# One encoder layer on one core: zeros on TensorE ahead of the opening, its first loads on two queues, smaller first pieces, and another order of the attention scores

## The chip, the cores and the metric

One core of one Trainium2 chip runs the whole layer as one program. The metric is the device time of one execution in microseconds. The kernel before took 1105.54 us (median of 3 runs, 1104.93 to 1105.83).

## The reference

The layer works on 256 tokens of width 2048, in float32. Cut to what matters here:

```python
h = rms_norm(x, attn_norm)
proj = h @ w_in                       # 2048 x 6152
qa, ka, va, fa, qb, kb, vb = split(proj)
# group A, 8 heads of 128: c = cumsum(log_sigmoid(fa + b_forget)) over the tokens
logits = qa . ka / sqrt(128) + c[t] - c[s]      # s <= t, then softmax, then @ va
# group B, 8 heads: stick-breaking attention from qb, kb, vb
x = x + concat(rms_norm(out_a), rms_norm(out_b)) @ w_out
x = x + conv_ffn(rms_norm(x))         # up, causal convolution of width 3, SiLU gate, down
```

`rms_norm` divides each token by the root of its mean square and multiplies the columns by a weight. The kernel multiplies by the weight first (as a scale per row of the transposed tokens) and divides by the root at the end of a projection.

## The kernel before, in words

**Arithmetic.** Every large product is done in three passes of matmuls on operands rounded to float32r: weights are cut into a high part `w_hi` (a cast, mostly on ScalarE) and a rest `w_lo` (a subtraction on VectorE), tokens into the two halves of `hT`. The passes are high by high, high by the token's rest, and the weights' rest by high. Small products, such as the attention scores, use plain float32 operands.

**Steps.** The program is a list of steps, each of one weight piece. The main loop at the end of `hybrid_layer` (L1270) runs over the steps n; at n it asks for the weights of step n + 6 (`LOAD`, a transfer on SyncE's queue into one of five buffers `w_raw`), lets the cast and subtraction of step n + 2 be written (`SPLIT`), and writes the matmuls of step n. Each engine, and SyncE's queue, works strictly in the order in which this was written.

**The opening** (`opening`, L322) computes the first 688 columns of the values of group A into four PSUM banks (`acc_v`: two halves of 344 columns by two blocks of 128 tokens). It goes through the 16 tiles of 128 columns of x in nine pieces: two of one tile, then seven of two tiles (`sizes`, L325). For each piece
- `loads` asks for the weights (344 KB a tile, L236) and for the columns of x (`load_x`, L118; 128 KB a tile) listed in `x_loads`. All go on SyncE's queue, x's first piece ahead of the first weights;
- `tokens` transposes the tiles of x on TensorE (`transposed`, L174, into `ps_x`), writes the two halves of `hT` on ScalarE and VectorE (`split_tokens`, L182 and L183) and casts and subtracts the weights (L242, L250). After every fourth tile ScalarE also sums the squares of 512 columns of x (`squares`, L190);
- `matmuls` issues 12 matmuls of 344 columns a tile (L369 for one-tile pieces, L267 for others), and behind them the `tokens` of the piece two further on.

The tokens of the first piece also need the norm's weights as columns: `prow` is loaded as rows on ScalarE's queue (L94, its first instruction), TensorE transposes it into `pp` (L167), VectorE copies it to `ga` (L168), which scales every `hT`. ScalarE's table load (L95) stands behind that transfer. The first two pieces are transposed together, ahead of the first matmul.

**The stage behind the opening** begins on TensorE with a second transpose of parameter rows (again `pp`, L167) and continues with the rest of the values.

**The scores of group A** (`fox_head`, L698): for each of 8 heads, three products accumulate into one bank `ps_s`: queries by keys for the first 128 tokens (L705), for the second 128 (L706), and a product that adds c[t] - c[s] in the form of a selecting row `headR` by the gates' sums `cR` (L707). VectorE then adds the mask and takes maxima (L712 to L715).

Of the kernel before, what the change touches and what calls it, by code (L numbers as in the profile page):

```python
# [9 lines left out]
F32 = mybir.dt.float32  # L10
# [5 lines left out]
P = 128  # L16
D = 2048
S = 256
NT = S // P
KT = D // P  # L20
# [16 lines left out]
C_COLS = C_MF + 4 * P  # L37

LOAD, SUM, SPLIT = 6, 4, 2
STAGGER = 3  # L40
FFN_PARTS = [(f, min(f + 8, NFT)) for f in range(0, NFT, 8)]

# [2 lines left out]
def hybrid_layer(  # L45
# [19 lines left out]
    nc = tc.nc  # L65
    act, dve = nc.scalar, nc.vector
# [16 lines left out]
    psb = ctx.enter_context(tc.tile_pool(name="psb", bufs=4, space=bass.MemoryType.PSUM))  # L83
# [7 lines left out]

    NC2 = 2 * NFT
    prow = const.tile([50, P], F32, name="prow")
    act.dma_start(prow[:KT, :], attn_norm[0].rearrange("(n p) -> n p", p=P))  # L94
    act.preload_act_table_set("natural_log_exp_and_others")  # L95
    cs = const.tile([P, C_MF], F32, name="cs")
    bf = const.tile([P, NH], F32, name="bf")
    pcol = const.tile([P, 50], F32, name="pcol")
    ga = const.tile([P, KT], F32, name="ga")
# [17 lines left out]
    def load_x(k, n, queue=nc.sync):  # L117
        queue.dma_start(x2[:, :, k * P : (k + n) * P], xp[:, :, k * P : (k + n) * P])  # L118

    ident = cs[:, C_ID : C_ID + P]  # L120
    make_identity(nc, ident)
    tri = cs[:, C_TRI : C_TRI + P]
    tri_one = cs[:, C_TRI : C_TRI + 2 * P]
# [41 lines left out]
    def columns(dst, rows, n):  # L165
        pp = psb.tile([P, 512], F32, name="pp", tag="t")
        nc.tensor.transpose(pp[:, :n], rows, ident[:n, :n])  # L167
        dve.tensor_copy(dst, pp[:, :n])  # L168

    def transposed(k, n=2):  # L170
        ps = psb.tile([P, 2, S], F32, name="ps_x", tag="t")
        for j in range(n):
            for t in range(NT):
                nc.tensor.transpose(  # L174
                    ps[:, j, t * P : (t + 1) * P], x2[:, t, (k + j) * P : (k + j + 1) * P], ident
                )
        return ps
# [67 lines left out]
    def split(raw, a, b):  # L245
        return subtracted(raw, *cast(raw, a * b, act.copy), a, b)
# [49 lines left out]
    VC = 344  # L296
# [25 lines left out]
    def opening():  # L322

        banks = []
        sizes = [1, 1] + [2] * 7  # L325
        starts = [sum(sizes[:i]) for i in range(len(sizes))]
        last = len(sizes) - 1
        x_loads = {0: (0, 2), 1: (2, 2), 2: (4, 2), 3: (6, 2), 4: (8, 4), 5: (12, 4)}
        mem = {}

        def piece(i):
            k0, n = starts[i], sizes[i]

            def loads():
                if i == 0:
                    load_x(*x_loads[i])
                mem["raw", i] = load(rows_of(wi, k0, n, V0, 2 * VC))
                if 0 < i < 6:
                    load_x(*x_loads[i])
                if i == 7:  # L340
                    load_parameters()

            def tokens():
                if n == 1 and i == 0:
                    columns(ga, prow[:KT, :], KT)
                    ps, mem["ps"] = (transposed(j, 1) for j in range(2))
                    hi, lo = cast(mem["raw", 0], 2 * VC, dve.tensor_copy)
                    split_tokens(ps, 0, ga, 1)
                    mem["parts", 0] = subtracted(mem["raw", 0], hi, lo, 1, 2 * VC)
                elif n == 1:  # L350
                    split_tokens(mem["ps"], 1, ga, 1)
                    mem["parts", 1] = split(mem["raw", 1], 1, 2 * VC)
                else:
                    split_tokens(transposed(k0), k0, ga)
                    mem["parts", i] = split(mem["raw", i], 2, 2 * VC)
                if k0 % 4 == 2:
                    squares(ss1, k0 // 4)
                if i == last:
                    ready.add("x")

            def matmuls():
                if i == 0:
                    banks.extend([bank_tile(f"acc_v{t}", 2 * j + t) for t in range(NT)] for j in range(2))
                if n == 1:
                    hi, lo = mem["parts", i]
                    for l, w in ((0, hi), (1, hi), (0, lo)):
                        for j in range(2):
                            for t in range(NT):
                                nc.tensor.matmul(  # L369
                                    banks[j][t][:, :VC], of_half(hT[:, k0], l, t),  # L370
                                    w[:, 0, j * VC : (j + 1) * VC], start=i == l == 0 and w is hi, stop=False,
                                )
                else:
                    for j in range(2):
                        in_three(
                            [banks[j][t][:, :VC] for t in range(NT)], mem["parts", i], 2, of_tokens(k0),
                            False, i == last, cut=slice(j * VC, (j + 1) * VC),
                        )
                if i + 2 <= last:
                    tokens_of[i + 2]()  # L380

            tokens_of.append(tokens)

            def follow():
                v = tile_of["v"] = at.tile([P, NT, WF], F32, name="vA", tag="v")
                for j in range(2):
                    for t in range(NT):
                        act.activation(
                            v[:, t, j * VC : (j + 1) * VC], banks[j][t][:, :VC], AF.Identity,
                            scale=rstd1[:, t : t + 1],  # L390
                        )
                    yield

            new_step(loads, None, tokens if i < 2 else None, matmuls, follow if i == last else None)

        tokens_of = []
        for i in range(len(sizes)):
            piece(i)
# [299 lines left out]
    def fox_head(h, half):  # L698
        q, k = tile_of[f"qA{half}"][:, h % 4, :], tile_of[f"kA{half}"][:, h % 4, :]
        v = tile_of["v"]  # L700
        yield
        yield
        ps = psb.tile([P, 512], F32, name="ps_s", tag="t")[:, : 3 * P].rearrange("p (a b) -> p a b", a=3)
        s0, s1 = ps[:, 0, :], ps[:, 1:3, :].rearrange("p a b -> p (a b)")
        nc.tensor.matmul(s0, q[:, :P], k[:, :P], start=True, stop=False)  # L705
        nc.tensor.matmul(s1, q[:, P:], k, start=False, stop=False)  # L706
        nc.tensor.matmul(  # L707
            ps.rearrange("p a b -> p (a b)"), headR[:, h : h + 1].to_broadcast([P, P]), cR, start=False, stop=True
        )
        started["fox"] += 1  # L710
        diagonal = ps[:, 0::2, :]
        dve.tensor_tensor(diagonal, diagonal, maskF, op=ALU.add)  # L712
        nm = small.tile([P, NT], F32, name="nm", tag="nm", bufs=4)
        dve.tensor_reduce(nm[:, 0:1], s0, axis=AX.X, op=ALU.max, negate=True)
        dve.tensor_reduce(nm[:, 1:2], s1, axis=AX.X, op=ALU.max, negate=True)  # L715
        yield
        yield
        l = small.tile([P, NT], F32, name="l", tag="l", bufs=4)
        pr = tmp.tile([P, 3, P], F32, name="pr", tag="pr")
        p0, p1 = pr[:, 0, :], pr[:, 1:3, :].rearrange("p a b -> p (a b)")  # L720
        act.activation(p0, s0, AF.Exp, bias=nm[:, 0:1], accum_out=l[:, 0:1])
        act.activation(p1, s1, AF.Exp, bias=nm[:, 1:2], accum_out=l[:, 1:2])
        rl = small.tile([P, NT], F32, name="rl", tag="rl", bufs=4)
        dve.reciprocal(rl, l)
        dve.tensor_scalar(p0, p0, rl[:, 0:1], None, op0=ALU.mult)
        dve.tensor_scalar(p1, p1, rl[:, 1:2], None, op0=ALU.mult)
        yield
        yield
        pt = psb.tile([P, 512], F32, name="ps_p", tag="t")[:, : 3 * P].rearrange("p (a b) -> p a b", a=3)
        for i in range(3):  # L730
            nc.tensor.transpose(pt[:, i, :], pr[:, i, :], ident)
        yield
        pT = tmp.tile([P, 3, P], F32, name="pT", tag="pT")
        act.copy(pT, pt)
        yield
        po = psb.tile([P, S], F32, name="ps_o", tag="t")
        hs = slice(h * HD, (h + 1) * HD)
        nc.tensor.matmul(po, v[:, 0, hs], pT[:, 0:2, :].rearrange("p a b -> p (a b)"), start=True, stop=False)
        nc.tensor.matmul(po[:, P:], v[:, 1, hs], pT[:, 2, :], start=False, stop=True)
        yield  # L740
        act.activation(oFox[:, h, :], po, AF.Identity, scale=g_fox[:, h : h + 1])
        sq = squared(po, 0, h)
        if sq is not None:
            dve.tensor_tensor(ssq[0], ssq[0], sq, op=ALU.add)
# [595 lines left out]
```

## Time and profile before

| | |
|---|---|
| median of 3 runs | 1105.54 us |
| the profiled execution | 1106.18 us |
| its span, first to last instruction | 1104.4 us |
| TensorE busy | 1092.8 us |
| VectorE busy | 902.9 us |
| ScalarE busy | 741.3 us |
| read from HBM | 252 MB, 230 GB/s over the span |

A page of the profile gives the busy time of each engine, the chain of work that ended last, and the costliest groups of instructions. Its other views list waits by who waited for whom, and instructions in order of time. PE is TensorE's matmul side, PEld its weight loads, DVE VectorE, ACT ScalarE, POOL GpSimd, SP SyncE; a q behind a name is its queue, where transfers are issued. In a row of the view by time stand the start (us from the first instruction), the duration, engine, line of the kernel, operation, output and inputs, and how many instructions are merged in the row; in brackets, the idle time ahead of it and what ended it. Matmuls overlap, so the time that one occupies TensorE is read from start to start.

### The profile page before, as it was taken

The page shows a single profiled execution, that of the slowest core. Times are in us where ns is not written, and L with a number is a line of the kernel's source. Part 1 is how long each engine was busy: PE and PEld are TensorE (multiplying, and loading weights), DVE is VectorE, ACT ScalarE, POOL GpSimd, SP SyncE. Part 2 cuts the span into 40 slices and gives each one's busy share as a digit, 9 for nine tenths or more (in the row PEclk, how much of TensorE's full clock was granted, in tenths as well). Part 3 has the DMA queues.
Part 4 walks back from the last instruction along what each step waited for, and adds up shares of the span by engine and source line. Part 5 has one row for each costly group of instructions (what it writes and reads, how often), then busy time and mean ns, then how long its engine had stood idle before and what let it go on. Part 6 is the DMA issues. An engine that isn't in the chain of part 4 may idle for free.

```text
span 1104.4 us, 14415 instructions
## 1 busy us (share of the span) xinstructions
PE 1092.8 (99%) x5666; PEld 941.5 (85%) x5666; DVE 902.9 (82%) x860; ACT 741.3 (67%) x923; POOL 55.1 (5%) x50
## 2 busy tenths in 40 slices
PE   8999999999999999999999999999999999999998
PEld 7988888888878888888888888888888888888886
DVE  4666888878897576679988998889898898879996
ACT  5745786667666567666767767766776667666762
POOL 0000000000100000000000010000000000000000
PEclk9999999999999999999999999999999999999999
DMA  8856877869777366557979598995979789795994
GB/s 303 285 192 190 262 184 241 208 189 265 255 191 264 125 206 202 185 166 174 316 201 289 203 267 250 249 300 160 301 208 277 237 230 303 197 317 168 287 263 139
DMA packets 174220, 255.35 MB, mean 231 GB/s; under 512 B 4408, under 2 KB 98378, under 8 KB 174154
## 3 DMA queue, kind: packets, MB, share of 16 engines
q1 hardware_dynamic: 152282, 210.26, 56.1%
q0 software_dynamic: 21696, 44.04, 22.6%
q8 instruction: 44, 0.72, 0.3%
q14 instruction: 22, 0.18, 0.0%
q10 hardware_dynamic: 176, 0.14, 0.0%
HBM read 252.33 MB, written 2.10 MB: 230 GB/s over the span
## 4 chain that ended last, share of the span: by engine, by line
PE 92%; DVE 5%; ACT 1%; issue 1%; DMA 0%; DVEq 0%; SPq 0%; ACTq 0%
PE pu L1089 43%; PE bank_a L267 16%; PE bank_b L267 9%; PE acc_o L267 5%; PE bank_c L267 5%; PE bank_p L267 4%; PE acc_v L267 4%; PE acc L267 2%; DVE w_lo L250 2%; PE bank_e L267 2%; ACT w_hi L242 1%; PE ps_x L174 1%; PE ps_h L627 0%; DMA w_raw<-in_w_in_dram 0%; PE acc_v L369 0%
## 5 line engine op out<-in xcount | busy, mean ns | idle before, releaser
L250 DVE TENSOR_TENSOR w_lo<-w_raw,w_hi 128x2048 fp32r<-128x2048 f32 (+2 forms) x246 | 551.9, 2246 | 147.5 <-ACT w_hi L242 146.8
L242 ACT CAST w_hi<-w_raw 128x2048 fp32r<-128x2048 f32 (+2 forms) x245 | 460.2, 1879 | 223.5 <-PE pu L1089 92.7
L1089 PE MATMUL pu<-hT,w_hi 128*128 128x512 f32 x1408 | 334.8, 390 | 0.7 <-ACT w_hi L242 0.7
L1089 PEld LDWEIGHTS pu<-hT,w_hi 128*128 128x128 f32 x1408 | 262.5, 188 | 54.8 <-ACT w_hi L242 1.2
L1089 PEld LDWEIGHTS pu<-hT,w_lo 128*128 128x128 f32 x1408 | 180.6, 191 | 7.0
L1089 PE MATMUL pu<-hT,w_lo 128*128 128x256 f32 x1408 | 182.8, 283 | 0.0
L1019 ACT ACTIVATE tap<-up,ccol 128x256 f32<-128x256 f32 x176 | 74.6, 495 | 0.0
L1138 POOL DMA_DIRECT2D w_raw<-in_w_down_dram x30 | 38.5, 1284 | 720.2 <-DVE w_raw L1156 317.7
L267 PE MATMUL bank_a<-w_hi,hT 128*128 128x512 f32 x160 | 40.7, 396 | 0.0
L267 PE MATMUL bank_b<-w_hi,s 128*128 128x512 f32 x160 | 40.1, 392 | 0.3 <-DVE xb L1111 0.3
L267 PE MATMUL bank_a<-w_hi,g 128*128 128x512 f32 x160 | 40.0, 392 | 0.0
L267 PE MATMUL bank_a<-w_hi,s 128*128 128x512 f32 x160 | 40.0, 392 | 0.0
L267 PEld LDWEIGHTS bank_a<-w_hi,hT 128*128 128x128 f32 x160 | 29.2, 188 | 5.6
L267 PEld LDWEIGHTS bank_b<-w_hi,s 128*128 128x128 f32 x160 | 28.9, 189 | 5.7 <-issue 0.5
L267 PEld LDWEIGHTS bank_a<-w_hi,s 128*128 128x128 f32 x160 | 28.9, 189 | 5.2
L267 PEld LDWEIGHTS bank_a<-w_hi,g 128*128 128x128 f32 x160 | 28.9, 189 | 5.3
L1012 ACT ACTIVATE gate<-up,ccol 128x256 f32<-128x256 f32 x44 | 24.0, 594 | 12.5 <-DVE s L1065 7.4
L1024 DVE TENSOR_TENSOR gate<-gate,tap 128x512 f32<-128x512 f32 x44 | 30.3, 689 | 2.5 <-ACT tap L1019 0.2
L1024 DVE TENSOR_TENSOR val<-val,tap 128x512 f32<-128x512 f32 x44 | 30.3, 689 | 2.3
L1005 DVE TENSOR_TENSOR up<-t,R 128x512 f32<-128x512 f32 x44 | 30.5, 692 | 1.5
L267 PE MATMUL acc_o<-w_hi,oSb 128*128 128x512 f32 x128 | 31.3, 396 | 0.0
L267 PE MATMUL acc_v<-w_hi,hT 128*128 128x344 f32 x176 | 31.2, 323 | 0.0
(269 smaller groups left out, 1392.4 us busy)
## 6 DMA issues: line engine op xcount, KB each, us to landing
w_raw<-in_w_up_dram SPq DMA_DIRECT2D x88, 1024.0 KB, 6.2
w_raw<-in_w_down_dram SPq DMA_DIRECT2D x44, 1024.0 KB, 7.0
w_raw<-in_w_in_dram SPq DMA_DIRECT2D x40, 1024.0 KB, 5.7
w_raw<-in_w_down_dram POOLq DMA_DIRECT2D x30, 1024.0 KB, 9.7
w_raw<-in_w_out_dram SPq DMA_DIRECT2D x16, 1024.0 KB, 7.5
w_raw<-in_w_in_dram POOLq DMA_DIRECT2D x8, 1024.0 KB, 9.7
w_raw<-in_w_in_dram SPq DMA_DIRECT2D x11, 688.0 KB, 7.7
xb<-in_x_dram POOLq DMA_DIRECT2D x4, 512.0 KB, 9.2
```

Source lines behind the costliest of these rows:

```text
L174: nc.tensor.transpose(ps[:, j, t * P : (t + 1) * P], x2[:, t, (k + j) * P : (k + j + 1) * P], ident)
L242: copy(hi[:, :n], raw[:, :n])
L250: dve.tensor_tensor(lo[:, :n], raw[:, :n], f32(hi[:, :n]), op=ALU.subtract)
L267: nc.tensor.matmul(o, lhs(i, l, t), r[:, i, :] if cut is None else r[:, i, cut], start=starts and j == 0, stop=stops and j == 3 * n - 1, s ...
L1005: dve.tensor_tensor(u[:, :, 2:], t2, R, op=ALU.mult)
L1012: act.activation(a[:, j, :], u[:, j, 2:], AF.Identity, scale=ccol[:, 2, f : f + 1], bias=ccol[:, 3, f : f + 1],)
L1019: act.activation(taps[w][:, j, :], u[:, j, w : w + S], AF.Copy, scale=ccol[:, w, f : f + 1])
L1024: dve.tensor_tensor(a, a, tap, op=ALU.add)
L1089: nc.tensor.matmul(acc[:, j, S:] if low else acc[:, j, :], (lo if low else hi)[:, i, j * P : (j + 1) * P], hT[:, k, 0, :] if low else hT[: ...
L1138: nc.gpsimd.dma_start(mem[weights].rearrange("p (a b) -> p a b", a=4), plus, accum_op=ALU.add)
```

## The change

Five edits, four of them in the opening.

1. VectorE sets 128 columns of the tile `junk` to zero at the start, and a new function `idle(n)` lets TensorE multiply them by themselves n times into a bank that nobody reads (`WARM = 7, 4`): seven ahead of the columns of `prow`, four behind the transposes of the first two tiles.
2. x's first piece goes on ScalarE's queue, with `prow` and the table load behind it; the first weights are then first on SyncE's queue.
3. The opening has eleven pieces: six of one tile, then five of two (`sizes`). The loads of x keep their sizes and are spread over pieces 0, 2, 4, 6, 7 and 8.
4. `tokens` is written once for both sizes; squares still come after every fourth tile, and the parameters' loads still stand with tiles 12 and 13.
5. In `fox_head` the gates' product is first and opens the accumulation; the two products of queries and keys follow.

```diff
+WARM = 7, 4
...
-    act.dma_start(prow[:KT, :], attn_norm[0].rearrange("(n p) -> n p", p=P))
-    act.preload_act_table_set("natural_log_exp_and_others")
...
+    dve.memset(junk[:, :P], 0.0)
     make_identity(nc, ident)
...
+    def idle(n):
+        ps = psb.tile([P, 2, S], F32, name="ps_i", tag="t")
+        for _ in range(n):
+            nc.tensor.matmul(ps[:, 0, :P], junk[:, :P], junk[:, :P], start=True, stop=True)
...
-        sizes = [1, 1] + [2] * 7
+        sizes = [1] * 6 + [2] * 5
...
-        x_loads = {0: (0, 2), 1: (2, 2), 2: (4, 2), 3: (6, 2), 4: (8, 4), 5: (12, 4)}
+        x_loads = {0: (0, 2), 2: (2, 2), 4: (4, 2), 6: (6, 2), 7: (8, 4), 8: (12, 4)}
...
                 if i == 0:
+                    load_x(*x_loads[i], act)
+                    act.dma_start(prow[:KT, :], attn_norm[0].rearrange("(n p) -> n p", p=P))
+                    act.preload_act_table_set("natural_log_exp_and_others")
+                elif i in x_loads:
                     load_x(*x_loads[i])
                 mem["raw", i] = load(rows_of(wi, k0, n, V0, 2 * VC))
-                if 0 < i < 6:
-                    load_x(*x_loads[i])
-                if i == 7:
+                if k0 == 12:
                     load_parameters()
...
             def tokens():
-                if n == 1 and i == 0:
+                if i == 0:
+                    idle(WARM[0])
                     columns(ga, prow[:KT, :], KT)
-                    ps, mem["ps"] = (transposed(j, 1) for j in range(2))
+                ps = transposed(k0, n)
+                if i == 1:
+                    idle(WARM[1])
...
-        nc.tensor.matmul(s0, q[:, :P], k[:, :P], start=True, stop=False)
-        nc.tensor.matmul(s1, q[:, P:], k, start=False, stop=False)
         nc.tensor.matmul(
-            ps.rearrange("p a b -> p (a b)"), headR[:, h : h + 1].to_broadcast([P, P]), cR, start=False, stop=True
+            ps.rearrange("p a b -> p (a b)"), headR[:, h : h + 1].to_broadcast([P, P]), cR, start=True, stop=False
         )
+        nc.tensor.matmul(s0, q[:, :P], k[:, :P], start=False, stop=False)
+        nc.tensor.matmul(s1, q[:, P:], k, start=False, stop=True)
```

What stands on TensorE at the start of the program (`pp` holds the columns of prow, `ps_x` transposed tokens, `acc_v` the values' banks), before:

```order
L1335 UNCONDITIONAL_BRANCH
L167 MATMUL pp<-cs,prow 128x16
L174 MATMUL ps_x<-cs,xa 128x128 x4
L369 MATMUL acc_v_168<-w_hi,hT 128x344
L369 MATMUL acc_v_169<-w_hi,hT 128x344
```

The same place in the changed program (`ps_i` is the bank of the zeros):

```order
L1343 UNCONDITIONAL_BRANCH
L173 MATMUL ps_i<-junk 128x128 x7
L167 MATMUL pp<-cs,prow 128x16
L179 MATMUL ps_x<-cs,xa 128x128 x4
L173 MATMUL ps_i<-junk 128x128 x4
L377 MATMUL acc_v_180<-w_hi,hT 128x344
L377 MATMUL acc_v_181<-w_hi,hT 128x344
```

The zeros stand ahead of the columns and between the transposes and the first matmul; what they surround keeps its order.

SyncE's queue at the start of the program, before (`xa` is x, `w_raw` a buffer of weights; 128x688 is one tile of weights, 128x2x688 two, 128x2x256 two tiles of x):

```order
L118 DMA xa<-in_x_dram 128x2x256
L236 DMA w_raw<-in_w_in_dram 128x688 x2
L118 DMA xa<-in_x_dram 128x2x256
L236 DMA w_raw<-in_w_in_dram 128x2x688
L118 DMA xa<-in_x_dram 128x2x256
L236 DMA w_raw<-in_w_in_dram 128x2x688
```

And in the changed program:

```order
L241 DMA w_raw<-in_w_in_dram 128x688 x2
L117 DMA xa<-in_x_dram 128x2x256
L241 DMA w_raw<-in_w_in_dram 128x688 x2
L117 DMA xa<-in_x_dram 128x2x256
L241 DMA w_raw<-in_w_in_dram 128x688 x2
L117 DMA xa<-in_x_dram 128x2x256
L241 DMA w_raw<-in_w_in_dram 128x2x688
```

The first piece of x is gone from this queue (it is now ScalarE's first instruction, with `prow` behind it), and one-tile loads of weights stand where two-tile loads stood.

The scores of the first head on TensorE, in the second unit of the projection, before (`bank_a` and `bank_c` are products of that unit):

```order
L267 MATMUL bank_a<-w_lo,hT 128x512 x4
L705 MATMUL ps_s<-kA_1118,qA_1150 128x128
L706 MATMUL ps_s<-kA_1118,qA_1150 128x256
L707 MATMUL ps_s<-cR,headR 128x384
L267 MATMUL bank_c<-w_hi,hT 128x512 x8
```

And in the changed program:

```order
L272 MATMUL bank_a<-w_lo,hT 128x512 x4
L713 MATMUL ps_s<-cR,headR 128x384
L716 MATMUL ps_s<-kA_1146,qA_1178 128x128
L717 MATMUL ps_s<-kA_1146,qA_1178 128x256
L272 MATMUL bank_c<-w_hi,hT 128x512 x8
```

The gates' product has moved from the third place to the first, between the same neighbours.

More of the change, by code (lines that the diff above doesn't have):

```diff
@@ L335, in loads @@
                 if i == 0:
+                    load_x(*x_loads[i], act)
+                    act.dma_start(prow[:KT, :], attn_norm[0].rearrange("(n p) -> n p", p=P))
+                    act.preload_act_table_set("natural_log_exp_and_others")
+                elif i in x_loads:
                     load_x(*x_loads[i])
                 mem["raw", i] = load(rows_of(wi, k0, n, V0, 2 * VC))
-                if 0 < i < 6:
-                    load_x(*x_loads[i])
-                if i == 7:
+                if k0 == 12:
                     load_parameters()
             def tokens():
-                if n == 1 and i == 0:
+                if i == 0:
+                    idle(WARM[0])
                     columns(ga, prow[:KT, :], KT)
-                    ps, mem["ps"] = (transposed(j, 1) for j in range(2))
+                ps = transposed(k0, n)
+                if i == 1:
+                    idle(WARM[1])
+                if i == 0:
                     hi, lo = cast(mem["raw", 0], 2 * VC, dve.tensor_copy)
-                    split_tokens(ps, 0, ga, 1)
+                split_tokens(ps, k0, ga, n)
+                if i == 0:
                     mem["parts", 0] = subtracted(mem["raw", 0], hi, lo, 1, 2 * VC)
-                elif n == 1:
-                    split_tokens(mem["ps"], 1, ga, 1)
-                    mem["parts", 1] = split(mem["raw", 1], 1, 2 * VC)
-                else:
-                    split_tokens(transposed(k0), k0, ga)
-                    mem["parts", i] = split(mem["raw", i], 2, 2 * VC)
-                if k0 % 4 == 2:
+                else:
+                    mem["parts", i] = split(mem["raw", i], n, 2 * VC)
+                if (k0 + n) % 4 == 0:
                     squares(ss1, k0 // 4)
```

## The prediction

> **What bounds the kernel now.** I read the page first, then TensorE's waits, then the rows of the opening in order of time.
>
> ```profile
> PE 1092.8 (99%) x5666; PEld 941.5 (85%) x5666; DVE 902.9 (82%) x860; ACT 741.3 (67%) x923; POOL 55.1 (5%) x50
> ...
> PE 92%; DVE 5%; ACT 1%; issue 1%; DMA 0%; DVEq 0%; SPq 0%; ACTq 0%
> ```
>
> TensorE is busy for 99% of the span and carries 92% of the chain that ended last. A change can only pay where TensorE waits, or where it works more slowly than it can.
>
> ```profile
> PE pp L167 <- DMA prow<-in_attn_norm_dram: 3.6, 1, 3.6
> PE acc_v L369 <- DVE w_hi L242: 1.0, 1, 1.0
> PE pu L1089 <- ACT w_hi L242: 0.7, 1, 0.7
> PE ps_o L781 <- ACT w L777: 0.7, 1, 0.7
> ```
>
> The two longest waits, 3.6 and 1.0 us, stand in the opening; no later one is above 0.7. No row of this view names the attention scores (ps_s). What moves the end of the opening should therefore move the end of the program by as much, since the loads and casts behind it are released by TensorE's own progress. The start of the opening:
>
> ```profile
> 0.74 0.43 SPq L118 DMA_DIRECT2D xa<-in_x_dram  x1
> 0.75 0.45 ACTq L94 DMA_DIRECT2D prow<-in_attn_norm_dram  x1
> ...
> 1.23 0.93 SPq L236 DMA_DIRECT2D w_raw<-in_w_in_dram  x2
> ...
> 3.61 0.26 PE L167 MATMUL pp<-cs,prow 16*128 16x16 f32 x1 [3.61 <-DMA prow<-in_attn_norm_dram]
> ...
> 4.00 1.12 PE L174 MATMUL ps_x<-cs,xa 128*128 128x128 f32 x4
> 4.73 0.90 ACT L182 ACTIVATE hT<-ps_x,ga 128x256 fp32r<-128x256 f32 x2 [2.22 <-PE ps_x L174]
> 5.46 0.52 DVE L242 CAST w_hi<-w_raw 128x688 fp32r<-128x688 f32 x1 [1.39 <-DMA w_raw<-in_w_in_dram]
> ...
> 6.13 2.63 PE L369 MATMUL acc_v<-w_hi,hT 128*128 128x344 f32 x8 [1.01 <-DVE w_hi L242]
> ...
> 8.56 1.35 PE L369 MATMUL acc_v<-w_lo,hT 128*128 128x344 f32 x4
> ...
> 9.71 1.05 PE L174 MATMUL ps_x<-cs,xa 128*128 128x128 f32 x4
> ...
> 10.41 2.30 PE L369 MATMUL acc_v<-w_hi,hT 128*128 128x344 f32 x8
> ...
> 12.55 0.79 PE L369 MATMUL acc_v<-w_lo,hT 128*128 128x344 f32 x4
> ...
> 15.21 0.61 PEld L267 LDWEIGHTS acc_v<-w_lo,hT 128*128 128x128 f32 x4 [0.39 <-DVE w_lo L250]
> ```
>
> Columns are start, duration, instruction, and the idle time before it. The first real matmul starts at 6.13 us. Read starts, not durations: four matmuls of 344 columns fill 8.56 to 9.71, which is 0.287 us each. Later the same matmuls go faster:
>
> ```profile
> 17.86 0.60 PE L174 MATMUL ps_x<-cs,xa 128*128 128x128 f32 x4
> ...
> 22.09 0.60 PE L174 MATMUL ps_x<-cs,xa 128*128 128x128 f32 x4
> ...
> 24.42 1.43 PE L267 MATMUL acc_v<-w_hi,hT 128*128 128x344 f32 x8
> ...
> 25.68 0.81 PE L267 MATMUL acc_v<-w_lo,hT 128*128 128x344 f32 x4
> ...
> 35.14 1.50 PE L267 MATMUL acc_v<-w_hi,hT 128*128 128x344 f32 x8
> ```
> ```profile
> 39.01 1.41 PE L267 MATMUL acc_v<-w_hi,hT 128*128 128x344 f32 x8
> ...
> 42.89 0.26 PE L167 MATMUL pp<-cs,prow 50*128 50x50 f32 x1
> ```
>
> Eight matmuls fill 24.42 to 25.68, 0.157 us each, with the same operands: TensorE starts slow and changes pace. Four transposes show the same two to one: 9.71 to 10.41 is 0.70 us, against 0.36 in steady pieces (4.23 us with transposes, 17.86 to 22.09, less 3.87 without, 35.14 to 39.01). The change of pace lies in the group at 10.41: its eight matmuls last 2.14 us to the next start instead of 2.30, so the last one or two were fast, and the switch was near 12.2 us, 6.1 us after steady work began at 6.13. Each microsecond at the slow pace costs 1 - 0.157/0.287 = 0.45 us. The opening ends at 42.89, where the parameter columns (pp) of the next stage begin.
>
> **The change, part by part.**
>
> *Pace and pieces.* All 16 tiles at the full pace, with transposes for 14 of them in between (two come ahead of the first matmul), take 7 x 4.23 + 3.87 = 33.5 us. Tiles 2 to 5 are now transposed in four groups of two instead of two of four; for that I add 0.1: 33.6. Now it is 42.89 - 6.13 = 36.76. The 3.15 us between them are the slow pace (6.1 x 0.45 = 2.75) and the 0.39 wait on w_lo at 15.21. One-tile pieces need ScalarE and VectorE to keep up:
>
> ```profile
> 7.08 0.77 ACT L242 CAST w_hi<-w_raw 128x688 fp32r<-128x688 f32 x1 [1.46 <-DMA w_raw<-in_w_in_dram]
> ...
> 7.88 0.88 DVE L250 TENSOR_TENSOR w_lo<-w_raw,w_hi 128x688 fp32r<-128x688 f32 x1 [0.33 <-ACT w_hi L242]
> ...
> 21.19 0.64 ACT L190 ACTIVATE junk<-xa 128x512 f32<-128x512 f32 x1
> ...
> 21.72 0.19 ACT L190 ACTIVATION_READ_ACCUMULATOR junk<-xa 128x1 f32 x1
> ```
>
> Per tile ScalarE does a scaling (0.47, half of the 0.90 row and a little) and a cast (0.77), 1.24 us of the tile's 2.1; VectorE 0.48 + 0.88 = 1.36. After tile 3 the squares add 2 x (0.64 + 0.19) = 1.66 to ScalarE; with two tiles' time, 4.2 us, for 2 x 1.24 + 1.66 = 4.14, they just fit. Stalls there cost between nothing and about twice the 0.39 of the w_lo row, 0.8; I take nothing. Weights and x come in time:
>
> ```profile
> w_raw<-in_w_in_dram SPq DMA_DIRECT2D x11, 688.0 KB, 7.7
> ```
> ```profile
> 6.10:9.50 3.40, 3.37 (x12) 3.40 (x13) 2.33 (x4) 0.77 (x1) 0.00 (x0) 1.00 1.03 369
> 9.50:12.10 2.60, 2.60 (x12) 2.54 (x11) 0.48 (x1) 0.75 (x2) 0.00 (x0) 1.00 1.04 389
> ```
>
> The first row ends with the median microseconds from issue to landing of a two-tile piece; in the others the last column is GB/s. A tile needs 344 KB of weights and 128 of x, in 2.1 us 230 GB/s; 369 to 389 flow. Five buffers now hold five tiles rather than eight; a load is asked for five pieces (10 us) ahead of use, and a two-tile piece lands 7.7 us after its issue. I cost this at nothing. (The clock column says 1.00 even here, so the pace is read from the starts.)
>
> *The zeros.* One float32 matmul is two instructions, as the scores' rows show:
>
> ```profile
> 143.07 0.38 PE L705 MATMUL ps_s<-kA,qA 128*128 128x128 f32 x2
> 143.29 0.60 PE L706 MATMUL ps_s<-kA,qA 128*128 128x256 f32 x2
> 143.54 0.52 PE L707 MATMUL ps_s<-cR,headR 128*128 128x384 f32 x1
> 143.90 2.01 PE L267 MATMUL bank_c<-w_hi,hT 128*128 128x512 f32 x8
> ```
>
> One of 128 columns occupies 143.07 to 143.29, 0.22 us at the full pace, so 0.43 at the slow one. They need only VectorE's memset, for which the nearest row is GpSimd's of the same size:
>
> ```profile
> 0.74 0.20 POOL masks.py:197 MEMSET cs<- 128x128 f32 x1 [0.29 <-POOLq L1325]
> ```
>
> So the zeros start near 1.0 us, and seven take 3.0, to 4.0. Ahead of nothing useful, they cost nothing until x and the norm's row (prow) are there. Behind them, in order, stand the columns, four transposes, four zeros, then the real work.
>
> *The two queues.* x's first piece stays first, but on ScalarE's queue; prow moves behind it; the first weights become first on SyncE's queue. TensorE saw prow at 3.61 and x at 4.00, VectorE the weights, second in one queue, at 5.46. In parallel both halves share the engines that move them: x and prow arrive between 4.00 (as now) and 5.46 (as if neither came before the sum of both). I take 4.4, nearer to the row of x itself. Then columns 0.2, transposes 0.70, four zeros 1.7 at the slow pace: the first real matmul starts at 4.4 + 2.6 = **7.0 us**, 0.9 later than now. At the full pace from the start it would be 5.7. The cast of the first weights (0.52) and ScalarE's scaling end before 7.0 and hide there. ScalarE's table load, 0.5 later, hides too: its first scaling ran at 4.73.
>
> *When the pace rises.* The trace has one switch, 6.1 us after steady work began. With zeros from 1.0 that is 7.1; I take it, so that only 0.1 us of real work is slow (0.05 us). It lies between 4.0 (at the end of the zeros) and 7.0 + 6.1 = 13.1 (zeros count for nothing). The Trainium skill ("TensorE: Matmul & The Clock Gate", Part 1) says that the clock is decided at the end of free-running windows of about 3.4 us, so that the switch's place varies from run to run; by it, an estimate, it would come somewhere from 4.4 to 7.8, on average 6.1, with the first real matmul at 6.6.
>
> *The scores.* Per head the same five instructions in another order, 0.83 us (143.07 to 143.90). The gates' product, now first, reads what was written long before:
>
> ```profile
> L450 ACT CAST cR<-pc x2: 259/312/365, 70.1 to 70.2; 64x128 fp32r<-64x128 f32 x1, 64x256 fp32r<-64x256 f32 x1
> ```
>
> At the pace of 344 columns its 384 would take 0.175; its row has 0.36 to the next start. Were that 0.19 lost or gained in all 8 heads, it would be 1.5 us either way. I take zero: the same switches between kinds of operand remain.
>
> *The sum.* End of the opening: 7.0 + 33.6 + 0.05 = 40.65 against 42.89, a gain of **2.24 us**. The profiled execution took 1106.18 us, 1.8 more than its span of 1104.4; the median of the three runs is 1105.54. I take the gain from the median: **1103.3 us**. About 0.2% (2.2 us) is what a measurement of this kernel tells from no change, so the forecast lies right at that bound.
>
> **The rivals.**
>
> *Early pace.* The switch comes by 4.4 and x at 4.0: columns, transposes and zeros take half, the real work starts near 5.5 and lasts 33.6: 39.1, a gain of 3.8 us, 1101.8; with one of the two conditions alone, about 1102.5. For it: the zeros begin 3 us ahead of any work now. Against: the one switch took 6.1 us. Chance 0.10.
>
> *The interruption counts.* A wait of 0.4 us for prow and then columns and transposes, 1.3 us together, start the count anew at 5.3: switch at 11.4, slow from 7.0 on, (11.4 - 7.0) x 0.45 = 2.0 lost: 42.6, a gain of 0.3, 1105.2. Against it, the stretch from 6.13 to 12.2 that led to the switch had 0.70 us of transposes inside. The Trainium skill (same page, Part 4) says that transposes don't count as activity in the same way; by that rule this rival is the outcome. The trace's stretch speaks against the rule but can't settle it. Chance 0.17.
>
> *It doesn't do what it says.* Zeros never raise the pace: switch at 13.1, 6.1 x 0.45 = 2.75 lost; 7.0 + 33.6 + 2.75 = 43.35, 0.5 slower, 1106.0. Chance 0.05.
>
> *Slower: prow late.* prow now stands behind x's 256 KB on one queue, and the columns, ScalarE's first scaling and everything on TensorE stand behind prow. Each microsecond after 4.4 moves the start by one. The gain is gone at 6.6; slower by 2.2 us needs prow at 8.9, which gives 1107.8. Against it: weights second in a queue were seen at 5.46. Chance 0.04.
>
> **How the numbers follow.** The forecast has 0.64; its own range is 1102.3 to 1104.3 (x from 4.0 to 5.0, the switch from 5.5 to 9). Of its 0.64 I put 0.38 below 1103.3. Faster: 0.38 + 0.10 = 0.48; within 0.2%: 0.26 + 0.17 + 0.05 = 0.48; slower 0.04. From 1102.0 to 1105.2 leaves out half of the early case, half of the interruption's, and the last two: 0.2.
>
> **What would show it.** Right: zeros from 1.0 to 4.0, columns near 4.4, the first real matmul near 7.0 with starts 0.157 apart, no wait inside the 16 tiles, pp of the next stage at 40.7, and 0.83 us for the scores of a head. A first matmul above 8 us breaks the queues' step; starts 0.287 apart beyond 9 us the zeros' step; waits on w_hi or w_lo between tiles 2 and 6 the pieces' step. It would be wrong altogether if waits past 43 us, not seen now, took the gain back.

## The result, and the profile after

The changed kernel takes **1108.23 us** (median of 14 runs, 1107.17 to 1108.95), the kernel before 1105.84 (14 runs, 1104.93 to 1106.11): a ratio of 1.002, interval 1.0013 to 1.0028. It is 2.4 us slower; 1103.3 was forecast. The profiled executions took 1107.53 and 1106.18 us, spans 1105.8 and 1104.4.

Busy times and the later waits stand almost as they were. The waits of TensorE, in total, times and longest:

```profile
PE pp L167 <- DMA prow<-in_attn_norm_dram: 2.0, 1, 2.0
PE ps_i L173 <- DVE junk L120: 1.1, 1, 1.1
PE pu L1097 <- ACT w_hi L247: 0.7, 1, 0.7
PE ps_o L789 <- ACT w L785: 0.7, 1, 0.7
PE acc_v L272 <- ACT w_hi L247: 0.5, 1, 0.5
```

The wait for prow is still the longest; a wait for w_hi inside the opening is new. The start of the changed kernel in order of time:

```profile
0.74 0.46 ACTq L117 DMA_DIRECT2D xa<-in_x_dram  x1
...
0.74 0.86 SPq L241 DMA_DIRECT2D w_raw<-in_w_in_dram  x2
...
1.06 3.36 PE L173 MATMUL ps_i<-junk 128*128 128x128 f32 x14 [1.06 <-DVE junk L120]
1.23 0.49 ACTq L342 DMA_DIRECT2D prow<-in_attn_norm_dram  x1
1.66 0.43 SPq L117 DMA_DIRECT2D xa<-in_x_dram  x1
...
2.12 1.18 SPq L241 DMA_DIRECT2D w_raw<-in_w_in_dram  x2
...
6.46 0.26 PE L167 MATMUL pp<-cs,prow 16*128 16x16 f32 x1 [2.05 <-DMA prow<-in_attn_norm_dram]
...
6.65 1.11 PE L179 MATMUL ps_x<-cs,xa 128*128 128x128 f32 x4
...
7.56 1.91 PE L173 MATMUL ps_i<-junk 128*128 128x128 f32 x8
...
9.12 2.20 PE L377 MATMUL acc_v<-w_hi,hT 128*128 128x344 f32 x8
...
11.16 0.79 PE L377 MATMUL acc_v<-w_lo,hT 128*128 128x344 f32 x4
...
11.79 0.38 PE L179 MATMUL ps_x<-cs,xa 128*128 128x128 f32 x2
```

The seven zeros run from 1.06 us as planned, then TensorE stands idle for 2 us until prow is there at 6.46 (3.61 before). The second zeros are still slow: eight instructions fill 7.56 to 9.12. The first real matmul starts at 9.12 instead of 6.13, and eight of them fill 2.04 us to the next start, 0.70 more than the same group needs at the full pace (1.34 in e1 below). At 0.45 us lost for each slow microsecond, the pace rose only near 10.7. Further on, at the first piece of two tiles, and at the end of the opening:

```profile
20.80 0.47 ACT L187 ACTIVATE hT<-ps_x,ga 128x256 fp32r<-128x256 f32 x1 [1.18 <-PE ps_x L179]
...
21.82 0.47 ACT L187 ACTIVATE hT<-ps_x,ga 128x256 fp32r<-128x256 f32 x1 [0.55 <-DVE hT L188]
...
22.20 1.33 ACT L247 CAST w_hi<-w_raw 128x1376 fp32r<-128x1376 f32 x1
...
22.48 0.60 PE L179 MATMUL ps_x<-cs,xa 128*128 128x128 f32 x4
...
23.57 1.24 PEld L272 LDWEIGHTS acc_v<-w_hi,hT 128*128 128x128 f32 x8 [0.74 <-ACT w_hi L247]
...
25.20 0.61 PEld L272 LDWEIGHTS acc_v<-w_lo,hT 128*128 128x128 f32 x4 [0.39 <-DVE w_lo L255]
```
```profile
44.41 0.26 PE L167 MATMUL pp<-cs,prow 50*128 50x50 f32 x1
```

The next stage's pp starts at 44.41 instead of 42.89. So the real work began 3.0 us later and was 1.5 us shorter (35.3 us against 36.8), and the opening ended 1.5 us later; the span grew by 1.4. From the transposes at 22.48 to the third pass at 25.20 it is 2.72 us, where the next piece needs 1.69. Nothing behind the opening took part. The difference of the medians, 2.4 us, is larger than that of the two profiled executions (1.35), of which one lies low in the changed kernel's range and the other just above the range of the 14 runs before.

### The profile page after: what moved, and what is told of

Its sections match the earlier page's. It is cut to its first block, busy times and chain, and to the rows that moved or that the text cites. A ratio compares the mean times of both kernels' runs of the same rounds, so it can differ in the third digit from the quotient of the medians.

```text
span 1105.8 us, 14474 instructions
## 1 busy us (share of the span) xinstructions
PE 1095.4 (99%) x5688; PEld 944.1 (85%) x5688; DVE 902.9 (82%) x863; ACT 741.0 (67%) x925; POOL 55.1 (5%) x50
## 4 chain that ended last, share of the span: by engine, by line
PE 92%; DVE 4%; ACT 1%; issue 1%; DMA 1%; ACTq 0%; DVEq 0%
PE pu L1097 43%; PE bank_a L272 16%; PE bank_b L272 9%; PE acc_o L272 5%; PE bank_c L272 5%; PE bank_p L272 4%; PE acc_v L272 3%; PE acc L272 2%; DVE w_lo L255 2%; PE bank_e L272 2%; ACT w_hi L247 1%; PE ps_x L179 1%; DMA w_raw<-in_w_in_dram 1%; PE ps_h L635 0%; DMA prow<-in_attn_norm_dram 0%
## 5 line engine op out<-in xcount | busy, mean ns | idle before, releaser
L272 PE MATMUL bank_p<-w_hi,hT 128*128 128x512 f32 x128 | 30.5, 390 | 0.0
```

The lines of the kernel that those rows point to most:

```text
L272: nc.tensor.matmul(o, lhs(i, l, t), r[:, i, :] if cut is None else r[:, i, cut], start=starts and j == 0, stop=stops and j == 3 * n - 1, s ...
```

## The experiments

All were timed in five rounds with the kernel before on the same chip (median 1105.84 with the first four, 1105.75 with the next, 1105.67 with the last), but e9, which ran once. Theory A: prow and x come late on ScalarE's queue, and the late start and the gap among the zeros follow from it. Rival B: the zeros cost more than they bring. C and D concern the pieces and the gap.

| kernel | what it has | us | ratio to before, interval |
|---|---|---|---|
| e1 | the change with the queues as before | 1104.40 | 0.9987 (0.9978 to 0.9996) |
| e2 | the change, prow ahead of x | 1106.66 | 1.0006 (0.9997 to 1.0015) |
| e3 | before + two queues | 1107.40 | 1.0017 (1.0008 to 1.0025) |
| e4 | before + zeros | 1104.79 | 0.9991 (0.9982 to 1.0000) |
| e5 | e1, all pieces of one tile | 1103.22 | 0.9983 (0.9974 to 0.9991) |
| e6 | before + six small pieces | 1105.77 | 1.0002 (0.9993 to 1.0011) |
| e7 | before + scores' order | 1105.76 | 1.0001 (0.9992 to 1.0010) |
| e8 | the change, 12 zeros in front | 1106.06 | 1.0003 (0.9994 to 1.0012) |
| e9 | the change, weights held back | 1105.81 | one run |
| e10 | e1 with ones for zeros | 1104.68 | 0.9990 (0.9981 to 0.9999) |
| e11 | e5 with two zeros for four | 1103.55 | 0.9981 (0.9972 to 0.9989) |

**The queues put back (e1).**

```diff
-                    load_x(*x_loads[i], act)
                     act.dma_start(prow[:KT, :], attn_norm[0].rearrange("(n p) -> n p", p=P))
                     act.preload_act_table_set("natural_log_exp_and_others")
+                    load_x(*x_loads[i])
```

> The changed kernel with the two queues as they were: prow and then the table load on ScalarE's queue, x's first piece on SyncE's queue ahead of the first weights. Zeros, one-tile pieces and the scores' order stay. Theory A (prow behind x on ScalarE's queue is what made the change slower): prow is seen by 3.6 us and x by 4.0, the zeros run without a gap to the real work at 6.5 to 7.0, the opening ends near 41, and the time is 1104 to 1105, below the kernel before. Rival B (the zeros cost more than they bring, the pace does not rise from them): the real work starts near 7.0 at the slow pace, the opening ends near 43, the time is 1106 to 1107.

1104.40 us: theory A. Its TensorE in order of time:

```profile
1.06 3.36 PE L173 MATMUL ps_i<-junk 128*128 128x128 f32 x14 [1.06 <-DVE junk L120]
4.34 0.28 PE L167 MATMUL pp<-cs,prow 16*128 16x16 f32 x1
4.56 1.11 PE L179 MATMUL ps_x<-cs,xa 128*128 128x128 f32 x4
5.47 1.15 PE L173 MATMUL ps_i<-junk 128*128 128x128 f32 x8
6.37 1.50 PE L377 MATMUL acc_v<-w_hi,hT 128*128 128x344 f32 x8
7.71 0.79 PE L377 MATMUL acc_v<-w_lo,hT 128*128 128x344 f32 x4
```

No row waits for a transfer. The second zeros fill 0.90 us where the changed kernel's take 1.56, so the pace rose among them, near 5.7, 4.6 us after the first zero. The first real group takes 1.34 us, the full pace. The opening ends at 40.97. Undoing this one edit turns 2.4 us slower into 1.4 faster.

**prow ahead of x on ScalarE's queue (e2).**

```diff
-                    load_x(*x_loads[i], act)
                     act.dma_start(prow[:KT, :], attn_norm[0].rearrange("(n p) -> n p", p=P))
+                    load_x(*x_loads[i], act)
                     act.preload_act_table_set("natural_log_exp_and_others")
```

> The changed kernel with prow ahead of x on ScalarE's queue. If it is prow's place behind x that costs (A1), prow is seen near 3.6 and x near 4.5, and the time is 1104 to 1105. If x itself comes late on ScalarE's queue beside two pieces of weights on SyncE's (A2), prow is seen early but x only near 5.7, the real work starts near 8.2, and the time is 1106.5 to 1107.5. Rival B expects no difference from the changed kernel, 1108.2.

1106.66 us, in the range of A2 and above that of A1. In the profiled execution x is late as well once prow stands ahead of it:

```profile
4.34 0.28 PE L167 MATMUL pp<-cs,prow 16*128 16x16 f32 x1
6.34 1.11 PE L179 MATMUL ps_x<-cs,xa 128*128 128x128 f32 x4 [1.72 <-DMA xa<-in_x_dram]
7.25 1.92 PE L173 MATMUL ps_i<-junk 128*128 128x128 f32 x8
8.82 2.35 PE L377 MATMUL acc_v<-w_hi,hT 128*128 128x344 f32 x8
```

The columns are ready by the end of the zeros, and TensorE then waits for x until 6.34, nearly as long as it waited for prow (1.72 and 2.05 us); the opening ends at 44.27 beside 44.41. So the place behind x is not what makes the queue late. The medians say less: e2 lies 1.6 us below the changed kernel, while the two profiled executions differ by 0.2 (1107.34, high among the runs of e2, and 1107.53, low among those of the changed kernel). What of the 1.6 the order is worth stays open.

**The two queues alone (e3).**

```diff
-    act.dma_start(prow[:KT, :], attn_norm[0].rearrange("(n p) -> n p", p=P))
-    act.preload_act_table_set("natural_log_exp_and_others")
...
                 if i == 0:
-                    load_x(*x_loads[i])
+                    load_x(*x_loads[i], act)
+                    act.dma_start(prow[:KT, :], attn_norm[0].rearrange("(n p) -> n p", p=P))
+                    act.preload_act_table_set("natural_log_exp_and_others")
```

> The kernel before with the two queues of the change alone. Theory A: prow is seen near 6.4 as in the changed kernel, the first real matmul starts near 8.3 instead of 6.1, and the time is 1107.5 to 1108.5. Rival B: prow late costs less than 0.5 us, the time is 1105.5 to 1106.3.

1107.40 us, 0.1 below the range that A gave, and clear of rival B. prow is seen at 6.55 and the first real matmul starts at 7.98:

```profile
6.55 0.25 PE L165 MATMUL pp<-cs,prow 16*128 16x16 f32 x1 [6.55 <-DMA prow<-in_attn_norm_dram]
...
7.98 2.66 PE L369 MATMUL acc_v<-w_hi,hT 128*128 128x344 f32 x8
```

Without zeros it is 1.43 us from prow to the first real matmul; in the changed kernel it is 2.66. Of the 3.0 us by which its real work starts later, 1.85 are thus the queues and 1.14 the zeros behind the transposes, which with prow late stand on the path at the slow pace.

**The zeros alone (e4).**

```diff
+    dve.memset(junk[:, :P], 0.0)
...
+    def idle(n):
...
+                    idle(7)
                     columns(ga, prow[:KT, :], KT)
                     ps, mem["ps"] = (transposed(j, 1) for j in range(2))
+                    idle(4)
```

> The kernel before with the zeros alone (7 ahead of the columns, 4 behind the first transposes). Theory A (zeros raise the pace when nothing interrupts them): the switch comes between 4.5 and 8 us, the real work starts at 6.5 to 7.0, the time is 1103.5 to 1104.5. Rival B (zeros do not raise it): the switch comes after 9 us, the start is 0.8 us later than before, the time is 1106 to 1107.

1104.79 us, at the side of A, though less fast than its range by 0.3:

```profile
5.47 1.45 PE L174 MATMUL ps_i<-junk 128*128 128x128 f32 x8
6.67 1.50 PE L377 MATMUL acc_v<-w_hi,hT 128*128 128x344 f32 x8
...
12.06 0.74 PE L273 MATMUL acc_v<-w_hi,hT 128*128 128x344 f32 x3 [0.51 <-ACT w_hi L248]
```

The first real group is fast. The last row is a wait for the weights of the first two-tile piece, which the kernel before does not have there (its w_hi group starts at 13.58 without a wait); it is large enough for the missing 0.3 us, but no run tests that it is their cause.

**All pieces of one tile (e5).**

```diff
-        sizes = [1] * 6 + [2] * 5
+        sizes = [1] * 16
...
-        x_loads = {0: (0, 2), 2: (2, 2), 4: (4, 2), 6: (6, 2), 7: (8, 4), 8: (12, 4)}
+        x_loads = {0: (0, 2), 2: (2, 2), 4: (4, 2), 6: (6, 2), 8: (8, 4), 12: (12, 4)}
...
-                                    w[:, 0, j * VC : (j + 1) * VC], start=i == l == 0 and w is hi, stop=False,
+                                    w[:, 0, j * VC : (j + 1) * VC], start=i == l == 0 and w is hi, stop=i == last and w is lo,
```

The last line closes the accumulation in the last piece, which now has one tile.

> The queues as before, zeros and the scores' order as changed, and all 16 tiles as pieces of one tile. In e1_loads_back TensorE stood 0.6 us for w_hi and 0.26 us for w_lo at the first piece of two tiles. Theory C (the tokens and weights of a two-tile piece are made ready in the time of one one-tile piece, which is too short at that one place): both waits go, the opening ends 0.7 to 0.9 us earlier than in e1_loads_back, the time is 1103.3 to 1103.9. Rival (small pieces cost as much in themselves): 1104.3 to 1105.

1103.22 us, 1.2 below e1; theory C. The waits inside the opening are gone from the list of waits, and 16 tiles take 33.3 us:

```profile
7.03 1.54 PE L377 MATMUL acc_v<-w_hi,hT 128*128 128x344 f32 x8
```
```profile
40.32 0.26 PE L167 MATMUL pp<-cs,prow 50*128 50x50 f32 x1
```

The profiled opening takes 1.3 us less than that of e1 from the first real matmul on (33.3 beside 34.6). This version beats both kernels. Not all of its gain reaches the time: the median of its spans, 1100.9 us, is 3.1 below that of the kernel before (1104.0), but in the median its runs take 2.3 us more than their spans where the others take 1.8, and those of e11 do the same. What the 0.5 us are, no trace shows.

**The small pieces alone (e6).**

```diff
-        sizes = [1, 1] + [2] * 7
+        sizes = [1] * 6 + [2] * 5
...
-        x_loads = {0: (0, 2), 1: (2, 2), 2: (4, 2), 3: (6, 2), 4: (8, 4), 5: (12, 4)}
+        x_loads = {0: (0, 2), 2: (2, 2), 4: (4, 2), 6: (6, 2), 7: (8, 4), 8: (12, 4)}
```

> The kernel before with the six pieces of one tile alone. Theory C: the wait at the first two-tile piece grows from 0.26 to 0.9 us, the time is 1106.2 to 1106.8. Rival (pieces of one tile start the work earlier): 1105.2 to 1105.7.

The `tokens` that the change wrote anew come along. 1105.77 us, between the two theories' ranges. The growth of the wait that C expects, 0.6 us, would be 0.06% of the time, and the interval is 0.09% to either side, so the time can't tell. The trace can: the first two-tile piece waits 0.50 us for w_hi, as in e1. What made up for it in this execution is an earlier rise of the pace, near 9.7 beside 12.2 before; as far as is known that is the luck of this execution. In the absence of zeros the six small pieces bring nothing that can be seen.

**The scores' order alone (e7).**

```diff
-        nc.tensor.matmul(s0, q[:, :P], k[:, :P], start=True, stop=False)
-        nc.tensor.matmul(s1, q[:, P:], k, start=False, stop=False)
...
-            ps.rearrange("p a b -> p (a b)"), headR[:, h : h + 1].to_broadcast([P, P]), cR, start=False, stop=True
+            ps.rearrange("p a b -> p (a b)"), headR[:, h : h + 1].to_broadcast([P, P]), cR, start=True, stop=False
...
+        nc.tensor.matmul(s0, q[:, :P], k[:, :P], start=False, stop=False)
+        nc.tensor.matmul(s1, q[:, P:], k, start=False, stop=True)
```

> The kernel before with the scores' order alone. All theories: five instructions a head in 0.83 us as before, the time is that of the kernel before, 1105.84, within 0.3 us. If the other order costs or saves the 0.19 us a head that the prediction gave as its bound: 1.5 us more or less.

1105.76 us against 1105.75: nothing. In its rows the gates' product starts where the first product of queries and keys did:

```profile
142.65 0.34 PE L705 MATMUL ps_s<-cR,headR 128*128 128x384 f32 x1
142.82 0.38 PE L708 MATMUL ps_s<-kA,qA 128*128 128x128 f32 x2
143.05 0.60 PE L709 MATMUL ps_s<-kA,qA 128*128 128x256 f32 x2
143.29 2.19 PE L267 MATMUL bank_c<-w_hi,hT 128*128 128x512 f32 x8
145.33 1.08 PE L267 MATMUL bank_c<-w_lo,hT 128*128 128x512 f32 x4
```

A single row's start misleads here, since a matmul may be entered before its predecessor is through (143.29). From the first score to the second pass of bank_c it is 2.68 us, and before it was 143.07 to 145.75, also 2.68.

**Zeros without a gap (e8).**

```diff
-WARM = 7, 4
+WARM = 12, 4
```

> The changed kernel with 12 zero matmuls instead of 7 ahead of the columns, which fill TensorE from 1.06 to 6.2 us at the slow pace, so that no gap is left until prow comes at 6.46. Theory D (the gap of 2.3 us is what kept the zeros from raising the pace): the pace rises between 4.5 and 8 us, the real work starts near 8 instead of 9.1 and is fast from its start, the time is 1106.7 to 1107.5. Rival (zeros do nothing, the transposes and real work raise the pace): the switch stays at 10 to 13 us, the time is 1108 to 1109.

1106.06 us, 2.2 below the changed kernel and even below D's range, though x lands as late as there (4.8 us after its issue, 4.7 there):

```profile
1.06 5.49 PE L173 MATMUL ps_i<-junk 128*128 128x128 f32 x24 [1.06 <-DVE junk L120]
6.61 0.22 PE L167 MATMUL pp<-cs,prow 16*128 16x16 f32 x1
6.76 0.66 PE L179 MATMUL ps_x<-cs,xa 128*128 128x128 f32 x4
7.26 1.06 PE L173 MATMUL ps_i<-junk 128*128 128x128 f32 x8
8.07 1.50 PE L377 MATMUL acc_v<-w_hi,hT 128*128 128x344 f32 x8
```

The transposes fill 0.50 us and the zeros behind them 0.81: the pace had risen by 6.8. The gap is what had kept it down in the changed kernel; e2, with a wait of 1.7 us, has its rise as late as that, near 10.7.

**x alone on ScalarE's queue (e9).**

```diff
+    held = []
...
         raw = wraw.tile([P, 2048], F32, name="w_raw", tag="w_raw")
+        if not held:
+            held.append(dve.tensor_copy(raw[:, :1], x2[:, 0, :1]))
```

> The changed kernel with SyncE's first weights held back (a one-column copy on VectorE that reads x's first piece and writes the weights' buffer ahead of their load), so that x and prow travel alone on ScalarE's queue. Its time is not the point. If x was late because the weights travel beside it (A2a), x is there near 4.0 and prow seen near 4.2. If ScalarE's queue itself is slow with a transfer of 256 KB (A2b), x is there only after 5 and prow is seen after 5.5.

A2a. VectorE, which waits for x, and SyncE's queue, which waits for VectorE:

```profile
3.73 0.15 DVE L243 COPY w_raw<-xa 128x1 f32<-128x1 f32 x1 [2.73 <-DMA xa<-in_x_dram]
3.91 0.86 SPq L245 DMA_DIRECT2D w_raw<-in_w_in_dram  x2
```

The table of transfers (queue, count, KB each, us from issue to landing) of this kernel, and of the changed one:

```profile
xa<-in_x_dram ACTq DMA_DIRECT2D x1, 256.0 KB, 3.0
...
prow<-in_attn_norm_dram ACTq DMA_DIRECT2D x1, 8.0 KB, 2.7
```
```profile
xa<-in_x_dram ACTq DMA_DIRECT2D x1, 256.0 KB, 4.7
```

Alone, x lands 3.0 us after its issue; beside the weights it takes 4.7, and prow, issued at 1.23 and seen at 6.46, 5.2 instead of 2.7. ScalarE's queue is not slow; what SyncE's queue sends beside it makes it late. The copy held back all of SyncE's transfers, so which of them costs how much (two pieces of weights, x's second piece, more weights) is not separated. With x and prow on time the pace rose near 6.3, and a wait of 1.1 us behind that, for w_hi, did not take it back: the first real group, at 8.05, takes 1.33 us. The Trainium skill ("DMA: Bandwidth & Descriptors", Issuing engines are not separate DMA queues) says that the two queues feed the same 16 DMA engines; these rows agree.

**Ones for zeros (e10).**

```diff
-    dve.memset(junk[:, :P], 0.0)
+    dve.memset(junk[:, :P], 1.0)
```

> e1_loads_back with ones in place of zeros in the tile that TensorE multiplies (nobody reads the product). If it is the matmuls and not their data that raise the pace: the time of e1_loads_back, 1104.4, within 0.6 us, the switch between 4.5 and 8 us. If zeros count for less: up to 1 us faster.

1104.68 us beside e1's 1104.40, within the expectation: ones do as well as zeros, as far as intervals of 0.09% to either side can tell. The profiled execution has its rise near 5.6, e1 near 5.7.

**Two zeros for four behind the transposes (e11).**

```diff
-WARM = 7, 4
+WARM = 7, 2
```

> e5_all_single with two zero matmuls instead of four behind the first transposes. In e5_all_single they ended at 7.03 us at the slow pace, while the first weights' cast was done near 6.0. If the pace still rises as early, the real work starts 0.3 to 0.9 us earlier and the time is 1102.6 to 1103.2; if the shorter stretch lets the switch slip, 1103.3 to 1104.

1103.55 us, in the second range, but 0.3 from e5 is less than the intervals can tell. The profiled execution shows no slip: its pace rose near 4.8 and its real work started at 5.88. That of e5 had its rise near 7.0 and lies 0.8 above its median, that of e11 0.4 below; of the other runs there are no traces, so where the pace rose in them is not known.

## Why the prediction was wrong

**The step that failed is the two queues.** "x and prow arrive between 4.00 (as now) and 5.46 ... I take 4.4" was sized from the rows of two transfers in one queue, x and then the first weights. It left out what else SyncE's queue sends by then: a second piece of weights right behind the first, x's second piece at 1.66 and more weights at 2.12. prow, last to be issued on ScalarE's queue, travels beside all of them. x landed near 5.4, at the upper edge of the range; prow was seen at 6.46, 1.0 beyond the upper bound and 2.1 beyond the value taken. Behind it the sum came out (2.66 us from prow to the first real matmul, 2.6 forecast), in part by luck: four transposes took 0.91 instead of 0.70, four zeros 1.56 instead of 1.7. e9 shows that SyncE's transfers make x and prow late, and e1 what the queues cost: 3.8 us of time.

**The pace was mis-sized through the same step.** Its rise was forecast at 7.1, 6.1 us after steady work began; it came near 10.7, because the gap of 2 us ended the steady work (e8: bridged, it came by 6.8). That cost the real work 0.70 us instead of 0.05. The rivals "the interruption counts" and "prow late" were given chances as if they excluded each other. They are one chain: a late prow makes the gap, and the gap holds the pace down. "prow late" alone gives its gain away at 6.6, which is about where prow came; with the gap on top the result is slower. The runs show the chain in the sum: the queues alone cost 1.6 us (e3) and the rest alone gains 1.4 (e1), which together would be 0.1 slower, but the change is 2.4 slower. The missing 2.3 us arise only when the two meet: a late prow holds the pace down and so leaves the slow zeros behind the transposes on the path.

**The pieces were costed at nothing, out of a range of up to 0.8 us, where they cost about 1.2.** ScalarE's time was added up for tiles 3 and 4, where it fits. The place that does not fit is the step from one-tile to two-tile pieces: the next piece's tokens and weights are made ready while the current one is multiplied, and there a two-tile piece has the time of a one-tile piece, 2.1 us. ScalarE needs 2.7 us for it (20.80 to 23.53): two scalings of 0.47, between them a wait of 0.55 for VectorE's half, which stands in no term of the sum, and a cast of 1.33. The matmuls of w_hi start right behind the cast; VectorE's subtraction of 1.59 us delays the third pass as well. The wait rows name 0.50 and 0.39 us of the loss. e5, where both are gone, is 1.2 us faster than e1 and takes 33.3 us for the 16 tiles, beside the 33.6 forecast.

**Right:** the zeros raise the pace (e4), and ones do it as well (e10); the forecast of 33.6 us for 16 tiles (33.3 in e5, with other pieces); the scores' order at nothing (e7); and that the opening's end moves the program's end one to one (1.5 and 1.4 us here, 1.9 and 2.1 earlier in e1). Added up for the opening, which ends 3.76 us later than forecast (44.41 for 40.65): 2.1 for the queues, 0.65 for the pace and 1.2 for the pieces, less the 0.3 by which 16 tiles were over-sized, 3.65 in all. With the queues left alone the same change is faster by 1.4 us (e1), not by the 2.24 forecast; its profiled opening ends at 40.97, 0.3 behind the forecast, as the real work starts 0.6 earlier and takes 1.0 longer.

**From one execution to the median.** The gain was taken from a median that lies 0.6 us below the profiled execution. The median after lies 0.7 above its own: 1.3 of the 4.9 us between forecast and median. The changed kernel's runs spread over 1.8 us, those before over 1.2. One profile shows one place of the rise. Up to 4.56 us TensorE's rows are the same in e1, e4, e5, e9, e10 and e11, and yet the distances of single starts put the rise near 5.7, 6.3, 7.0, 6.3, 5.6 and 4.8. The one place of 6.1 us behind steady work that the forecast of 7.1 rests on was thus one draw of several; all six lie within the 4.4 to 7.8 that the prediction put beside its 7.1. How much of the spread of the times comes from this, no run shows.

## What to carry to other kernels

A second queue did not spare its transfers the company of the first here: before putting the first input of a chain on it, count every transfer that the other queue has issued by then, and the small one that stands last. Filling an idle engine to raise its pace worked here where the filling ran on until the pace had risen, and failed where a wait of 2 us came before that, so size it by the latest arrival, not by the planned one. Where a pipeline changes its piece size, check the first larger piece, with the waits between the engines that make it ready, against the time of the last smaller one.

## What the runs showed of the hardware

The rise of TensorE's pace came 3.7 to 6.1 us after steady work began: in the zeros' runs 3.7 (e11) to 5.9 (e5) after 1.06, 4.2 in the changed kernel (from 6.46), 3.8 in e6 (from 5.87), 6.1 before (from 6.13). Equal work ahead of it does not fix the place. Zeros and ones do equally well (1104.40 and 1104.68 us). Transposes inside the stretch do not prevent it: in e1 they take 0.91 of the 4.6 us. They change pace themselves: four fill 0.91 us ahead of the rise in e1 and 0.50 behind it in e8. The Trainium skill ("TensorE: Matmul & The Clock Gate", Part 4) says that transposes don't count in the same way; whether they count for less, no run here separates. A wait of 2 us ahead of the rise does hold it up (e8 against the changed kernel, 2.2 us apart); a wait of 1.1 us behind it did not bring the slow pace back (e9).
